# Token sums in twelve steps between evictions, decay earlier, gates spread over the attention

## The chip, the cores and the metric

The kernel runs on one core of a Trainium2 chip. TensorE (PE) multiplies matrices, VectorE (DVE), ScalarE (ACT) and GpSimd (POOL) work on tiles, SyncE (SP) issues most DMAs. Each engine takes its instructions in one fixed order and waits at an instruction until what it reads is written and what it overwrites has been read. The metric is the device time of one execution in microseconds (us). A difference is given against the kernel before.

## The reference, cut to what matters

One layer of a decoder over 1024 tokens of width 1024. A combined projection feeds three mixers: FoX (4 heads, full causal attention with a learned decay), dilated windows (6 heads in 3 groups), and NSA (6 heads in 2 groups; compressed blocks, 8 selected blocks, a window of 512). Each mixer's output is projected, multiplied by a sigmoid gate and summed.

```python
h = rms_norm(x, norm1_g[l])
proj = h @ w_in[l] + b_in[l]          # q, k, v, decay, NSA gates, 3 x 1024 merge gates
y_a = fox_attention(...); y_b = dilated_attention(...); y_c = nsa_attention(...)
g = jax.nn.sigmoid(gates).reshape(B_, S, 3, D)
merged = (g[:, :, 0] * (y_a @ w_pa[l]) + g[:, :, 1] * (y_b @ w_pb[l])
          + g[:, :, 2] * (y_c @ w_pc[l]))
x = x + merged @ w_o[l]
x = x + conv_ffn(rms_norm(x, norm2_g[l]), ...)
# inside FoX: c = cumsum(log_sigmoid(f_logit)); s = q.k * scale + c[t] - c[s]
# inside NSA: kc, vc = gelu(blocks @ w1) @ w2; imp = p_c summed over blocks; top 8 blocks are kept
```

## The kernel before

All products are made in float32 accuracy from two parts, a rounded high part and the low remainder: `mm3` issues three matmuls (L283 to L285) for one product. A weight is loaded by SP (`wr`), its high part (`wh`, `bh`) cast by ScalarE, its low part (`wl`, `bl`) subtracted by GpSimd or VectorE. Two buffers each of `wr`, `wh`, `wl` go round.

The order of the stages is that of `run`. `phase0` norms and transposes the input into `hT` (high and low, two halves of 512 tokens). `proj_va` makes FoX's values and decay logits, `proj_vn` NSA's values and its gate logits, both with tokens as rows: eight token tiles each of 24 matmuls into one of two `dn` banks, evicted by VectorE to `tm` (L668), then cast by ScalarE (L675), its low part made by GpSimd (L676), and stored by SP (L678). `tok_weights` (L635) fills one pair of buffers `bh`, `bl`, so `proj_vn`'s weights follow `proj_va`'s last matmul. Between the two stands `token_sums` (L472 to L495): for the four pairs of row blocks it forms the sums T1 to T4 of a block scheme with fewer products, on 128x512 tiles, seven instructions on VectorE (L483 to L489) and two on GpSimd (L490, L491), and then splits each T into a cast by ScalarE (L493) and a remainder by VectorE or GpSimd (L494). `proj_pairs` uses them for the query, key and value projections; its weights are combined by GpSimd (`su`, L578 to L581) and split (L587, L588).

Fourteen DMAs that GpSimd issues (`dax`, `day`, `dac`, L1772 to L1774) put constant rows of the attention into DRAM buffers; they are released by `last_split`, the low part of the last token weights made so far.

After the pairs, `fox_decay` (L704) turns the decay logits `fa` into the cumulative log decay `fcc` (two activations, some ten VectorE instructions, two small matmuls), and twice `compress_in` and `compress` follow: a projection (KC, then VC), then 48 matmuls of 256 columns over the compression weights `cmp_k_w1` or `cmp_v_w1`.

Then the attention runs. A strip is 128 queries of one head against its keys: score matmuls into `S` (L785, L789; mask L787), row maximum by VectorE (L792), exponent by ScalarE (L800), scaling (L808 to L816), transposes (L857), splits (L863, L864), and products with the values (L886, L887). Ten FoX and dilated heads come first, then for each NSA group a selection (`nsa_select`, L1226: scores of compressed blocks L1242 to L1245, small VectorE instructions L1251 to L1286, transposes L1293, a store into `dax`, which the next loads read back into `q2`, the second operand of L789) and three heads. TensorE's order is written out by a planner, `Flow`: it follows strips and their later steps by a model of the engines, and where none is ready it takes a step of the filler. The filler, `dense_work` (L1317), makes the 24 merge gates (`gate`, L1306): each has 48 matmuls of 512 columns in two `dn` banks, a ScalarE eviction and a DMA. Gates 0 to 20 are taken as soon as there is room, 21 to 23 only behind the attention. Gates' weights come in the order of `weight_list` (L1325): KC, VC, gate 0, 1, and so on. `branch` (L1332) then reads the mixers' outputs (`yh` is cast at L1340), and the merge begins.

## Time and profile before

| what | value |
|---|---|
| median of three runs | 1807.32 us (1804.41 to 1808.73) |
| the profiled execution: time, span | 1807.93 us, 1806.2 us |
| TensorE busy, mean granted clock | 94% of the span, 0.98 |
| first matmul of the pairs, of the compression, of the strips | 104.20, 280.45, 339.50 us |
| last gate matmul, last attention matmul, first of the merge | 810.96, 940.14, 947.29 us |

A view by windows gives the busy time of every engine in a stretch; a view in order of time gives single instructions, and in brackets how long the engine had been idle before one and what released it. An order gives what stands behind what on an engine, and no times.

### The profile page before, as it was taken

The page shows a single profiled execution, that of the slowest core. Times are in us where ns is not written, and L with a number is a line of the kernel's source. Part 1 is how long each engine was busy: PE and PEld are TensorE (multiplying, and loading weights), DVE is VectorE, ACT ScalarE, POOL GpSimd, SP SyncE. Part 2 cuts the span into 40 slices and gives each one's busy share as a digit, 9 for nine tenths or more (in the row PEclk, how much of TensorE's full clock was granted, in tenths as well). Part 3 has the DMA queues.
Part 4 walks back from the last instruction along what each step waited for, and adds up shares of the span by engine and source line. Part 5 has one row for each costly group of instructions (what it writes and reads, how often), then busy time and mean ns, then how long its engine had stood idle before and what let it go on. Part 6 is the DMA issues. An engine that isn't in the chain of part 4 may idle for free.

```text
span 1806.2 us, 24845 instructions
## 1 busy us (share of the span) xinstructions
PE 1691.9 (94%) x8504; PEld 1395.2 (77%) x8504; DVE 1354.0 (75%) x2657; ACT 803.7 (44%) x1638; POOL 468.9 (26%) x334
## 2 busy tenths in 40 slices
...
GB/s 240 71 131 156 130 176 171 184 178 177 192 189 181 69 120 136 68 153 36 8 42 227 208 221 6 18 111 175 186 141 175 179 175 148 135 263 236 204 227 61
DMA packets 224325, 266.52 MB, mean 148 GB/s; under 512 B 20712, under 2 KB 160078, under 8 KB 223990
## 3 DMA queue, kind: packets, MB, share of 16 engines
...
q14 instruction: 60, 0.49, 0.1%
...
## 4 chain that ended last, share of the span: by engine, by line
PE 30%; DVE 15%; issue 5%; DMA 5%; ACT 3%; POOL 2%; SPq 0%; POOLq 0%; DVEq 0%; ACTq 0%
PE dn L284 4%; PE dn L283 4%; PE dn L285 4%; PE S L285 2%; PE S L284 2%; PE S L283 2%; DVE t L1556 2%; DVE u L1614 2%; PE T L284 2%; PE T L283 2%; PE T L285 2%; PE T L857 1%; DVE wl L1493 1%; DVE wh L1493 1%; DVE tl L864 1%
## 5 line engine op out<-in xcount | busy, mean ns | idle before, releaser
L271 POOL TENSOR_TENSOR wl<-wr,wh 128x1024 fp32r<-128x1024 f32 (+2 forms) x50 | 87.9, 1757 | 557.1 <-ACT wh L269 470.8
L283 PE MATMUL dn<-hTh,wh 128*128 128x512 f32 x444 | 179.7, 405 | 0.0
L284 PE MATMUL dn<-hTl,wh 128*128 128x512 f32 x444 | 174.4, 393 | 0.0
L285 PE MATMUL dn<-hTh,wl 128*128 128x512 f32 x416 | 164.0, 394 | 0.0
L800 ACT ACTIVATE p<-S,sm 128x384 f32<-128x384 f32 (+2 forms) x192 | 106.6, 560 | 88.9 <-DVE sm L796 66.6
L864 DVE TENSOR_TENSOR tl<-T,th 128x512 fp32r<-128x512 f32 (+2 forms) x202 | 115.7, 585 | 25.8 <-ACT th L863 24.8
L863 ACT CAST th<-T 128x512 fp32r<-128x512 f32 (+2 forms) x202 | 99.2, 508 | 75.4 <-PE T L857 72.6
L792 DVE TENSOR_REDUCE sm<-S 128x1 f32<-128x384 f32 (+2 forms) x192 | 98.0, 526 | 44.1 <-PE S L789 42.0
L857 PE MATMUL T<-ident,p 128*128 128x128 f32 x610 | 94.8, 279 | 12.1 <-DVE tl L864 5.6
L1556 DVE SCALAR_TENSOR_TENSOR t<-u,ccols,t 128x511 f32<-128x511 f32 (+1 forms) x88 | 96.9, 1101 | 7.5 <-ACT t L1551 6.4
L789 PE MATMUL S<-k,q 114*128 114x384 f32 (+6 forms) x240 | 96.5, 402 | 2.4 <-DMA k<-fcc 1.3
L886 PE MATMUL PV<-th,v 128*128 128x256 f32 (+1 forms) x362 | 95.1, 287 | 1.8 <-DVE yt L903 1.8
L785 PE MATMUL S<-k,q 128*128 128x384 f32 (+2 forms) x240 | 86.1, 359 | 8.4 <-ACT p L800 7.7
L284 PEld LDWEIGHTS dn<-hTl,wh 128*128 128x128 f32 x444 | 84.4, 190 | 12.3
L283 PEld LDWEIGHTS dn<-hTh,wh 128*128 128x128 f32 x444 | 84.3, 190 | 12.1 <-issue 0.6
L887 PE MATMUL PV<-tl,v 128*128 128x256 f32 (+1 forms) x362 | 90.2, 286 | 2.4 <-DVE tl L864 2.4
L285 PEld LDWEIGHTS dn<-hTh,wl 128*128 128x128 f32 x416 | 78.5, 189 | 16.9
L857 PEld LDWEIGHTS T<-ident,p 128*128 128x128 f32 x610 | 70.7, 142 | 21.9 <-DVE p L816 5.0
L887 PEld LDWEIGHTS PV<-tl,v 128*128 128x128 f32 x362 | 70.4, 195 | 6.3 <-DVE tl L864 3.9
L886 PEld LDWEIGHTS PV<-th,v 128*128 128x128 f32 x362 | 70.2, 194 | 5.9 <-DVE yt L903 3.5
L1481 POOL TENSOR_TENSOR su<-wr 128x512 f32<-128x512 f32 x20 | 31.2, 1560 | 142.1 <-DMA wr<-w_up 91.9
L816 DVE TENSOR_SCALAR p<-p,sm,gsig 128x256 f32<-128x256 f32 (+3 forms) x144 | 65.6, 486 | 1.2
...
## 6 DMA issues: line engine op xcount, KB each, us to landing
...
```

The lines of the kernel that those rows point to most:

```text
L283: nc.tensor.matmul(out, st[0], mv[0], start=first, stop=False)
L284: nc.tensor.matmul(out, st[0], mv[1], start=False, stop=False)
L285: nc.tensor.matmul(out, st[1], mv[0], start=False, stop=last)
L789: nc.tensor.matmul(ps[:, 0:wn * P], q[1][0:R, qs], k[1][0:R, cs], start=False, stop=True)
L792: nc.vector.tensor_reduce(mx if ci == 0 else sm[:, 1:2], v, AX.X, ALU.max, negate=True)
L800: nc.scalar.activation(pt[:, 0:m, :].rearrange("p a b -> p (a b)"), v, AF.Exp, bias=mx, accum_out=sm[:, 2 + ci:3 + ci])
L857: nc.tensor.transpose(ps[:, n * P:(n + 1) * P], b, self.ident)
L863: nc.scalar.copy(th[:, cs], ps[:, cs])
L864: nc.vector.tensor_tensor(tl[:, cs], ps[:, cs], th[:, cs].bitcast(F32), ALU.subtract)
L886: nc.tensor.matmul(unit.pv[:, oc], w, th[:, cs], start=first and i == 0, stop=False)
L887: nc.tensor.matmul(unit.pv[:, oc], w, tl[:, cs], start=False, stop=e)
L1556: nc.vector.scalar_tensor_tensor(o, i, cw[2 - sh], o, ALU.mult, ALU.add)
```

## The change

The sums become a generator that yields after T1, after T2, and after T3 with T4, four times: twelve steps. `proj_tok` calls one behind each token tile, released by the tile's eviction and its low part; what is left after both projections is drained then. `constants2` moves ahead of the first projection and `fox_decay` between the two; the fourteen GpSimd issues follow the second projection's last split. Gate 0 and gate 1 are run between `compress_in` and `compress`, and the weight list follows. Gates 2 to 20 are let into the attention only as its strips progress: each strip adds its key blocks and 3 to `prog`, and gate f waits until `prog * 21` has reached `total * (f - 3)`. Gates 21 to 23 stay closed while strips remain.

```diff
@@ -161,6 +161,7 @@
         self.S, self.T, self.PV, self.dn = Ring(3), Ring(2), Ring(1), Ring(2)
         self.p, self.th = Ring(8), Ring(3)
         self.marks = set()
+        self.prog, self.total = 0, 1
         self.vq, self.tq, self.later, self.stores = [], [], [], []
         self.running = False
         self.loads, self.strips, self.filler, self.fn = [], None, None, None
@@ -468,9 +469,9 @@
             self.done = evac(hh, ps)
             F.dn.give(self.done)
 
-    def token_sums(self, pool):
-
-        nc, B = self.nc, {}
+    def token_sums(self, pool, B):
+
+        nc = self.nc
         v, g = nc.vector.tensor_tensor, nc.gpsimd.tensor_tensor
         for n, i, k in (("B11", 0, 0), ("B21", 0, 4), ("B12", 1, 0), ("B22", 1, 4)):
             B[n] = tuple(x[:, k:k + 4] for x in self.hT[i])
@@ -480,19 +481,27 @@
             f = {n: tuple(x[:, i].bitcast(F32) for x in B[n]) for n in B}
             tt = [self.st.tile([P, 2, 512], F32, t) for t in (("sh", "sl"), ("f4", "f4"))[i % 2]]
             r = {n: tt[x // 2][:, x % 2] for x, n in enumerate(("T1", "T2", "T3", "T4"))}
+
+            def split(n, e):
+                nc.scalar.copy(B[n][0][:, i], r[n])
+                e(B[n][1][:, i], r[n], f[n][0], ALU.subtract)
+
             v(r["T1"], f["B12"][0], f["B11"][0], ALU.subtract)
             v(r["T1"], r["T1"], f["B12"][1], ALU.add)
             v(r["T1"], r["T1"], f["B11"][1], ALU.subtract)
+            split("T1", v)
+            yield
             v(r["T2"], f["B22"][0], r["T1"], ALU.subtract)
             v(r["T2"], r["T2"], f["B22"][1], ALU.add)
+            split("T2", g)
+            yield
             v(r["T3"], r["T2"], f["B11"][0], ALU.subtract)
             v(r["T3"], r["T3"], f["B11"][1], ALU.subtract)
             g(r["T4"], f["B21"][0], r["T2"], ALU.subtract)
+            split("T3", v)
             g(r["T4"], r["T4"], f["B21"][1], ALU.add)
-            for n, e in (("T1", v), ("T2", g), ("T3", v), ("T4", g)):
-                nc.scalar.copy(B[n][0][:, i], r[n])
-                e(B[n][1][:, i], r[n], f[n][0], ALU.subtract)
-        return B
+            split("T4", g)
+            yield
 
     def out_qk(self, side, dst, r=1, scale=1.0):
 
@@ -665,25 +674,30 @@
                 self.mm3(ps[:, 0:n], self.toks(self.hT, k, t),
                          (hi[:, k, 0:n], lo[:, k, 0:n]), k == 0, k == 7)
             tm = rawp.tile([P, 274], F32, "tm")
-            nc.vector.tensor_tensor(tm[:, 0:n], ps[:, 0:n], bc[:, 0:n], ALU.add)
-            evac(t, tm)
+            out = nc.vector.tensor_tensor(tm[:, 0:n], ps[:, 0:n], bc[:, 0:n], ALU.add)
+            low = evac(t, tm)
+
+            if self.steps:
+                with self.tc.issue_after(out.ins), self.tc.issue_after(low.ins):
+                    next(self.steps, None)
 
     def v_store(self, t, tm, c0, nh, dsts):
         nc = self.nc
         vs = self.st.tile([P, 4, P], F32R, "v4")
         tv = tm[:, c0:c0 + nh * 64].rearrange("p (h d) -> p h d", h=nh)
         nc.scalar.copy(vs[:, 0:nh, 0:64], tv)
-        nc.gpsimd.tensor_tensor(vs[:, 0:nh, 64:128], tv, vs[:, 0:nh, 0:64].bitcast(F32), ALU.subtract)
+        low = nc.gpsimd.tensor_tensor(vs[:, 0:nh, 64:128], tv, vs[:, 0:nh, 0:64].bitcast(F32), ALU.subtract)
         for (dst, h0, hn) in dsts:
             nc.sync.dma_start(dst[:, t * P:(t + 1) * P, :].rearrange("h p d -> p h d"),
                               vs[:, h0:h0 + hn, :].bitcast(F32))
+        return low
 
     def proj_va(self):
         nc = self.nc
 
         def evac(t, tm):
-            self.v_store(t, tm, 0, 4, [(self.dv["a"], 0, 4)])
             nc.vector.tensor_copy(self.fa[:, :, t], tm[:, 256:260])
+            return self.v_store(t, tm, 0, 4, [(self.dv["a"], 0, 4)])
 
         self.proj_tok(self.va, 260, evac)
 
@@ -692,8 +706,8 @@
         gl = self.early.tile([P, NT, 18], F32, "gl")
 
         def evac(t, tm):
-            self.v_store(t, tm, 0, 4, [(self.dv["s"], 0, 2), (self.dv["w"], 2, 2)])
             nc.vector.tensor_copy(gl[:, t, :], tm[:, 256:274])
+            return self.v_store(t, tm, 0, 4, [(self.dv["s"], 0, 2), (self.dv["w"], 2, 2)])
 
         self.proj_tok(self.tok_weights([(C_VSL, 128), (C_VWN, 146)], 274), 274, evac)
         e = self.early.tile([P, NT, 18], F32, "ge")
@@ -703,7 +717,7 @@
 
     def fox_decay(self):
 
-        nc, ap = self.nc, self.ap
+        nc, ap = self.nc, self.early
         t = lambda n: ap.tile([P, 4, NT], F32, n)
         cm = ap.tile([P, 256], F32, "cm")
         nc.sync.dma_start(cm, self.a["c_main"][:, K_TRI:K_TRI + 256])
@@ -721,7 +735,7 @@
         ps = self.psA.tile([P, 512], F32, "T")
         nc.tensor.matmul(ps[0:32, 0:P], lf.rearrange("p h i -> p (h i)"), tri, start=True, stop=False)
         nc.tensor.matmul(ps[0:32, 0:P], lp.rearrange("p h i -> p (h i)"), ones, start=False, stop=True)
-        cc = ap.tile([32, 4, P], F32R, "fcc")
+        cc = self.nsac.tile([32, 4, P], F32R, "fcc")
         nc.scalar.copy(cc[:, 0], ps[0:32, 0:P])
         nc.vector.tensor_tensor(cc[:, 1], ps[0:32, 0:P], cc[:, 0].bitcast(F32), ALU.subtract)
         nc.vector.tensor_scalar(cc[:, 2], cc[:, 0].bitcast(F32), -1.0, None, ALU.mult)
@@ -762,6 +776,7 @@
 
         nc, ap, F = self.nc, self.ap, self.F
         n = kb1 - kb0 + 1
+        F.prog += n + 3
         sm = ap.tile([P, 8], F32, "sm")
         qs = slice(qi * P, (qi + 1) * P)
         mx, ls = keep or (sm[:, 0:1], sm[:, 4:5])
@@ -1314,19 +1329,22 @@
 
         yield from self.dense_steps(evac)
 
-    def dense_work(self):
-
-        for f in range(24):
+    def dense_work(self, done):
+
+        F = self.F
+        for f in range(done, 24):
             if f == 21:
 
                 yield lambda: INF if self.F.attending else 0.0
+            else:
+
+                yield lambda f=f: INF if F.prog * 21 < F.total * (f - done - 1) else 0.0
             yield from self.gate(f)
 
     def weight_list(self):
         win = self.a["w_in"][0]
         w = lambda c, sc=None: ([win[:, c:c + P]], 8, P, sc)
-        out = [w(C_KC), w(C_VC)]
-        out += [w(C_G + f * P) for f in range(24)]
+        out = [w(C_KC), w(C_G), w(C_VC)] + [w(C_G + f * P) for f in range(1, 24)]
         return out
 
     def branch(self, pool, ys, br):
@@ -1765,16 +1783,20 @@
         self.psA = Pool(self, "psA", {"dn": 2, "S": 3, "T": 2, "PV": 1}, space=PSUM)
         self.start()
         self.phase0()
+        self.constants2()
+        tp = Pool(self, "sums", {})
+        B = {}
+        self.steps = self.token_sums(tp, B)
         self.proj_va()
-        self.constants2()
+        self.fox_decay()
+        self.proj_vn()
         with self.tc.issue_after(self.last_split.ins):
             for i in range(12):
                 nc.gpsimd.dma_start(self.dax[i], a["c_ax"][i])
             nc.gpsimd.dma_start(self.day, a["c_ay"])
             nc.gpsimd.dma_start(self.dac, a["c_ac"])
-        tp = Pool(self, "sums", {})
-        B = self.token_sums(tp)
-        self.proj_vn()
+        for _ in self.steps:
+            pass
         self.early.close()
         pp = Pool(self, "pairs", {})
         self.proj_pairs(B, pp)
@@ -1784,11 +1806,13 @@
                                      "yt": 4, "ce": 2, "csm": 4, "pb": 2})
         self.F = F = Flow()
         self.wspec, self.wloaded, self.wready = self.weight_list(), [], []
-        F.strips, F.filler = self.attention(), self.dense_work()
-        self.fox_decay()
+        F.total = 1138
+        F.strips, F.filler = self.attention(), self.dense_work(2)
         self.ap2 = Pool(self, "att2", {"p": 8})
         for i in range(2):
             fq = self.compress_in(i)
+            for _ in self.gate(i):
+                pass
             self.compress(i, fq)
         with self.tc.manual_schedule(engines={mybir.EngineType.PE}):
             F.run(True)
```

Three places of the orders, before and after. The first is GpSimd between the last token sums and the pairs' `su`; `T2l`, `T4l` are remainders of the sums (L494, after L487), `v` the low parts of token tiles (L676, after L689), L490 and L491 (after L500, L502) sums. Before:

```order
L490 TENSOR_TENSOR f_153_742<-hTh_1_78,f_152_741 128x512
L491 TENSOR_TENSOR f_153_742<-f_153_742,hTl_2_79 128x512
L494 TENSOR_TENSOR T2l_679<-f_152_741,T2h_678 128x512
L494 TENSOR_TENSOR T4l_683<-f_153_742,T4h_682 128x512
L676 TENSOR_TENSOR v_164_813<-tm_811,v_164_813 128x4x64
```

After:

```order
L1795 DMA dax_24_129<-c_ax 16x3200
L1795 DMA dax_25_130<-c_ax 16x3200
L689 TENSOR_TENSOR v_169_801<-tm_798,v_169_801 128x4x64
L500 TENSOR_TENSOR sl_677<-hTh_1_78,sh_676 128x512
L689 TENSOR_TENSOR v_172_842<-tm_839,v_172_842 128x4x64
L502 TENSOR_TENSOR sl_677<-sl_677,hTl_2_79 128x512
L1795 DMA dax_26_131<-c_ax 16x3200
L487 TENSOR_TENSOR T4l_445<-sl_677,T4h_444 128x512
L1795 DMA dax_27_132<-c_ax 16x3200
L689 TENSOR_TENSOR v_177_882<-tm_879,v_177_882 128x4x64
L1795 DMA dax_28_133<-c_ax 16x3200
L1795 DMA dax_29_134<-c_ax 16x3200
```

Sums, splits and the issues, which stood ahead of the sums, now stand between the low parts of the second projection's tiles.

The second is TensorE in the compression of the values; `S` is the product with the compression weights `k`, `dn_3095` gate 2. Before:

```order
L283 MATMUL S_2835<-k_474_2837,p_2817 128x256
L284 MATMUL S_2835<-k_475_2838,p_2817 128x256
L285 MATMUL S_2835<-k_474_2837,p_2818 128x256
L283 MATMUL S_2835<-k_477_2856,p_2821 128x256
L284 MATMUL S_2835<-k_478_2857,p_2821 128x256
L285 MATMUL S_2835<-k_477_2856,p_2822 128x256
```

After:

```order
L286 MATMUL S_2957<-k_489_2978,p_2883 128x256
L284 MATMUL dn_3095<-hTh_1_78,wh_2895 128x512
L285 MATMUL dn_3095<-hTl_2_79,wh_2895 128x512
L286 MATMUL dn_3095<-hTh_1_78,wl_2896 128x512
L284 MATMUL S_2957<-k_492_2997,p_2886 128x256
L284 MATMUL dn_3095<-hTh_1_78,wh_2895 128x512
L285 MATMUL dn_3095<-hTl_2_79,wh_2895 128x512
L286 MATMUL dn_3095<-hTh_1_78,wl_2896 128x512
L284 MATMUL dn_3095<-hTh_1_78,wh_2895 128x512
L285 MATMUL dn_3095<-hTl_2_79,wh_2895 128x512
```

Before, the 48 matmuls of that product stood in a row; now gate 2 stands between them, and gates 0 and 1 ahead of the two products.

The third is TensorE in the second selection; `dn` are gate matmuls, `T` transposes of the selection (L1293, after L1308), L785 to L789 (after L800 to L804) the first strips behind it, L1257 to L1260 scores of compressed blocks. Before:

```order
L283 MATMUL dn_10395<-hTh_3_80,wh_10305 128x512
L1293 MATMUL T_8622<-ident_82,s_1755_8607 16x128 x4
L785 MATMUL S_8643<-k_1714_8393,q_1758_8632 128x256
L787 LDWEIGHTS identb_648
L787 MATMUL S_8643<-mk_645,identb_648 128x128
L284 MATMUL dn_10395<-hTl_4_81,wh_10305 128x512
L285 MATMUL dn_10395<-hTh_3_80,wl_10306 128x512
L283 MATMUL dn_10395<-hTh_3_80,wh_10305 128x512
```

After:

```order
L1260 MATMUL S_8404<-k2c_398,q_1695_8206 128x256
L1257 MATMUL S_8404<-k1c_397,q_1694_8205 128x256
L1258 LDWEIGHTS identb_392
L1258 MATMUL S_8404<-mk_389,identb_392 128x64
L1260 MATMUL S_8404<-k2c_398,q_1695_8206 128x256
L1308 MATMUL T_8439<-ident_82,s_1737_8424 16x128 x4
L800 MATMUL S_8460<-k_1696_8210,q_1740_8449 128x256
L802 LDWEIGHTS identb_392
L802 MATMUL S_8460<-mk_389,identb_392 128x128
L804 MATMUL S_8460<-k_1697_8211,q_1741_8450 128x256
L800 MATMUL S_8471<-k_1696_8210,q_1740_8449 128x256
L802 LDWEIGHTS identb_392
```

The gate matmuls around the transposes are gone: scores, transposes and the first strips follow one another, and the first gate matmul comes four strips later.

## Rows read from the trace of the kernel before

**Rows 1.** The page, part 1: span, then busy us, share and instructions of each engine.

```profile
span 1806.2 us, 24845 instructions
...
PE 1691.9 (94%) x8504; PEld 1395.2 (77%) x8504; DVE 1354.0 (75%) x2657; ACT 803.7 (44%) x1638; POOL 468.9 (26%) x334
```

**Rows 2.** By stage: stretch, us, busy PE PEld DVE ACT POOL (instructions), PEclk, DMA, GB/s.

```profile
45.00:104.20 59.20, 36.07 (x225) 33.12 (x223) 47.77 (x55) 16.32 (x31) 39.98 (x29) 0.77 0.29 78
...
280.45:339.50 59.05, 51.28 (x255) 41.34 (x253) 36.86 (x74) 22.24 (x32) 9.59 (x9) 0.94 0.70 170
339.50:811.00 471.50, 463.05 (x2744) 387.71 (x2744) 329.63 (x1090) 244.62 (x641) 63.54 (x37) 0.99 0.55 150
811.00:940.30 129.30, 99.44 (x650) 81.70 (x648) 107.68 (x318) 73.76 (x210) 1.00 (x1) 0.95 0.06 17
```

**Rows 3.** TensorE in order of time, second token projection and pairs: start, us, line, operation.

```profile
89.69 0.29 PE L283 MATMUL dn<-bh,hTh 128*128 128x274 f32 x1
...
92.87 0.29 PE L284 MATMUL dn<-bl,hTh 128*128 128x274 f32 x1
...
107.17 0.39 PE L283 MATMUL S<-hTh,wl 128*128 128x512 f32 x1
...
108.98 0.39 PE L285 MATMUL S<-hTh,wl 128*128 128x512 f32 x1
```

**Rows 4.** Front in order of time, [idle before <-releaser]; last GpSimd's issues by tile, ns least/median/most.

```profile
39.95 0.68 DVE L483 TENSOR_TENSOR sh<-hTh,hTh 128x512 f32<-128x512 f32 x1
...
58.18 1.76 DVE L489 TENSOR_TENSOR f<-f,hTl 128x512 f32<-128x512 f32 x1
...
84.31 0.59 PE L283 MATMUL dn<-bh,hTh 128*128 128x274 f32 x1 [5.89 <-DVE tm L668]
...
99.32 0.73 POOL L676 TENSOR_TENSOR v<-tm,v 128x256 fp32r<-128x256 f32 x1 [2.32 <-ACT v L675]
...
106.13 1.29 POOL L578 TENSOR_TENSOR su<-wr 128x512 f32<-128x512 f32 x1
...
110.88 0.51 PE L285 MATMUL S<-T3h,wl 128*128 128x512 f32 x1 [0.66 <-DVE wl L588]
...
L1772 POOL DMA_DIRECT2D dax<-c_ax x12: 486/493/671, 21.5 to 38.5; - x12
```

**Rows 5.** Compression: TensorE's waits (us, times, longest), ScalarE in time, a stretch.

```profile
PE S L283 <- ACT k L1188: 2.1, 1, 2.1
...
329.43 1.04 ACT L1188 CAST k<-q 128x1024 fp32r<-128x1024 f32 x1 [3.92 <-DMA q<-cmp_v_w]
...
330.00:340.00 10.00, 7.33 (x32) 6.27 (x32) 3.23 (x5) 2.31 (x5) 0.94 (x1) 0.66 0.62 155
```

**Rows 6.** Attention by stretch, columns as in rows 2, cut where heads begin.

```profile
339.50:544.83 205.33, 202.19 (x1202) 170.20 (x1202) 142.33 (x463) 120.09 (x322) 29.57 (x16) 0.98 0.69 184
544.83:590.60 45.77, 45.77 (x262) 38.44 (x260) 29.72 (x128) 15.41 (x33) 9.16 (x7) 1.00 0.69 190
...
717.65:763.93 46.28, 45.82 (x292) 38.42 (x291) 35.13 (x103) 27.18 (x74) 4.35 (x2) 1.00 0.23 66
763.93:803.47 39.54, 35.94 (x215) 29.57 (x214) 26.76 (x132) 12.19 (x31) 5.13 (x6) 1.00 0.73 188
...
847.50:890.20 42.70, 32.54 (x228) 26.51 (x227) 37.49 (x116) 26.00 (x76) 0.00 (x0) 1.00 0.07 21
890.20:940.30 50.10, 39.07 (x258) 32.35 (x256) 41.69 (x124) 28.71 (x83) 0.00 (x0) 0.94 0.03 7
```

**Rows 7.** Second selection's way through memory: the stretch, and VectorE's next instruction.

```profile
793.00:803.47 10.47, 9.06 (x42) 6.98 (x42) 0.00 (x0) 2.26 (x4) 0.74 (x1) 1.00 0.67 192
...
803.89 0.79 DVE L792 TENSOR_REDUCE sm<-S 128x1 f32<-128x128 f32 x2 [10.92 <-PE S L789]
```

**Rows 8.** End of the attention: TensorE's first merge matmul, and the stretch before it.

```profile
947.29 0.80 PE L283 MATMUL S<-yh,wh 128*128 128x512 f32 x1 [6.74 <-ACT yh L1340]
...
940.30:950.00 9.70, 2.92 (x8) 1.72 (x8) 3.07 (x4) 3.50 (x4) 0.00 (x0) 0.68 0.55 181
```

## The prediction

> **What bounds the kernel now.** The page's first part comes first: TensorE is busy 94% of the span of 1806.2 us [rows 1]. The profiled execution took 1807.93 us in all, 0.6 above the median of 1807.32 (1804.41 to 1808.73), so the sum is made against 1807.9 and the difference is left out. A share of 94% is a mean, so I cut the span at the first matmul of each stage [rows 2]. Four stages then look different. From 45 to 104.2 us (end of the first token projection, the token sums, the second token projection) VectorE works 47.8 of 59.2 us, TensorE 36.1, and at a mean granted clock of 0.77. In the compression stage TensorE is busy 51.3 of 59.05. In the attention up to 811 it is full. From 811 to 940.3, where no gate work is left, it is busy 99.4 of 129.3, and VectorE 107.7.
>
> Busy times of matmuls hold modelled ends, so I also price the order. Eight steps of 512 columns took 1.81 us, 25 of 274 columns 3.18 [rows 3]: 0.226 and 0.127 us each, or 0.416 ns a column and 13 ns a matmul. Transposes are counted twice, as a choice. One gate (48 matmuls of 512 columns) is then 10.9 us. Priced like that, the attention before is 514.5 us of work in 600.8: 442.8 in 471.5 up to 811 (6% over), 71.6 in 129.3 behind it (80% over). What the gates are worth as filler is the difference between these two rates.
>
> **Front: the sums.** Before, VectorE makes the sums in one block that starts at 39.95; the second projection's first evictions are queued behind it, and TensorE stands 5.89 us until the first of them has freed a bank, at 84.31 [rows 4]. A sum of 128x512 takes VectorE 0.68 us alone and 1.76 beside a GpSimd sum or split. The work stays: 28 sums and 8 splits on VectorE, 8 and 8 on GpSimd, 16 casts. By the order 12 of VectorE's stand behind the second projection's first eviction, where 2 stood: 10 at 0.7 to 1.8 us, 7 to 18 us, have left its way. Against that come the decay instructions, now ahead of the first such eviction: 7 adds and some eight small VectorE instructions, two activations and two matmuls, some 4 us by chained waits; and the second weights' low parts share one buffer with the first's, so they wait for a last first-projection tile that now comes later. I take the first eviction 6 to 9 us earlier, at 75 to 78. On SP the constants' and the decay's loads go ahead of the second weights, which wait for their buffers anyway: nothing.
>
> That does not move the pairs as far, because GpSimd becomes late. The 14 `dax`, `day`, `dac` issues, 0.493 us median [rows 4], ran in idle GpSimd time before the block; now they stand between the sums and the preparation of the pair weights `su`, which starts at 106.13 before, and the third product's low weight is waited for at 110.88 [rows 4], so nothing is slack there. Queue after: 8 low parts of 0.73, 7 sums and splits of about 1.7 (1.76 is the nearest row), 14 issues of 0.49 = 5.8 + 11.9 + 6.9 = 24.6 us from some 77 to 79, so `su` starts at 102 to 104: **3 us earlier**. Bounds: with the issues in gaps 7 us earlier; with each tile waiting for the one before, 3 later.
>
> A rule speaks against the new place of the issues. In the row they take 0.49 median and 0.67 at most, the twelve `dax` between 21.5 and 38.5, where VectorE splits the normed input. The Trainium skill ("DMA: Bandwidth & Descriptors", section SWDGE vs HWDGE vs iDMA) says that GpSimd writes descriptors into SBUF state from which a VectorE instruction in a two-port mode locks it out. The row shows little of it; what it would do is the third rival.
>
> **Compression.** Before, TensorE waits there for the cast of the compression weights, 2.1 us in one piece, ScalarE having waited 3.92 for their DMA, and the stretch 330 to 340 runs at a mean clock of 0.66 [rows 5]. By the order it holds 141 dense matmuls and 96 of 256 columns: 31.9 + 11.5 + about 1 = 44.4 us of work in 59.05, so 14.6 lost. After: gates 0 and 1 whole and 45 matmuls of gate 2, that is 237 dense, 96 more, 21.7 us; two stand in the very places of these waits. Work 66.1. I take 4 us still lost (the first strips' loads, the tail of the second compression, which has little filler): stage 70, 11 longer, for 21.7 us of gates that leave the attention: **net -10.8**. Bounds: nothing lost -14.5; half of the loss left -7.5; none recovered, a rival. The gates' result tiles share two buffers with the compression's inputs; the wait for their stores is hidden by a gate's 10.9 us. The decay's move out is in this too.
>
> **Attention.** Without the 21.7 us the old one would be 579.1. After, by the order: gate work in the ten FoX and dilated heads 91 (107 before), in the two selections 7.4 and 0 (before 30.5 and 12.4, and more behind the second), and two gates, 21.7, in each of the six NSA heads (before 33, 37, 18, 13, 0 and 0).
> - FoX and dilated: 205.3 us for 188.5 of work before [rows 6], 1.09; after 173.2, at the same rate 189.
> - NSA heads: the old head nearest to the new ones (25.3 of strips, 17.7 of gates, 717.65 to 763.93) took 46.28 for 43.0, 1.076 [rows 6]. After: strips of 157.4 in all and 130.2 of gates, 287.6, times 1.076 = 309.5. The last two took 42.7 and 50.1 without gates [rows 6]; they would take 52 and 56 with 21.7 each, so their gates cost 15 of 43.
> - Selections: 45.8 and 39.5 before. In the second VectorE works 26.8 us, all of it ahead of 793 [rows 6, 7], then stands 10.92 while the selection is stored and read back into `q2`; TensorE meanwhile worked on gates, 9.06 of 10.47 us at full clock [rows 7]. After there is no filler in the second, little in the first; the VectorE work and the round trip stay: 39.5 each, 79.
>
> Sum 577.5 against 579.1: **-1.6**. So the gain of the filled tail is nearly paid back by two selections that stand empty. On SP the gates' weight loads, now later, stand among the heads' loads and wait for a buffer: nothing while a gate lies between two of them, up to a gate's 10.9 us at one head if not. Bounds: rates of 1.04 and 1.03 in heads give 555; the other end is the second rival.
>
> **End.** Before, the first merge matmul waits 6.74 us for the casts of the last attention output [rows 8]; ten matmuls of gate 23 now fill a part of that hole. It ends at the same cast: 0 (-2; +3 if the merge weights, whose buffers the gates now hold longer, come late).
>
> **Sum.** -3 - 10.8 - 1.6 + 0 = -15.4: **1792.5**; with what the bounds of the terms add alike, 1778 to 1803.
>
> **Rivals.** *First, the spread works everywhere at the rate of the full body:* only 3% are lost outside the selections: (173.2 + 287.6) x 1.03 + 79 = 553.6, -25.5; total 1807.9 - 3 - 10.8 - 25.5 = 1768.6. For it: TensorE was busy 202.2 of 205.3 us in the first ten heads and throughout the first selection [rows 6]. Against: VectorE needs 37.5 of 42.7 us in a head without gates [rows 6].
>
> *Second, slower: the gate by progress leaves holes.* After, 14 stretches of strips alone exceed 3 us of work, 90.7 us together (before 6, 92.9). If all run like the old tail, 1.8 x 90.7 + (492.8 - 90.7) x 1.065 = 591.5, 12.4 more than 579.1. And TensorE leaves each selection cold: in the hole of 6.7 us before the merge the clock falls, 0.68 over 940.3 to 950, the lower level of 1.2 GHz for two thirds of it [rows 8]. At two thirds of 10 us a stretch, half the rate costs 3.4 us each, 6.8 for both, by the 0.66 of [rows 5] over one such stretch. Together +19.2: 1807.9 - 3 - 10.8 + 19.2 = 1813.3. It decides from some +14 in the attention. Against: most of these stretches are short and have gates on both sides. The Trainium skill ("TensorE: Matmul & The Clock Gate", section HAM oscillation) has the same rule, that repeated holes make each following stretch start cold; the trace agrees at the merge (0.68) and shows full clock where gates fill the round trip.
>
> *Third, the front's issues are stretched* like VectorE's sums beside GpSimd, 1.76 for 0.68, 2.6 times: 14 x 0.8 = 11 more on GpSimd, `su` 8 late instead of 3 early: 1792.5 + 11 = 1803.5.
>
> *Fourth, the change does not do what it says in the compression:* weights bound the stage, the gates only lengthen it by their 21.7: 1792.5 + 10.8 = 1803.3.
>
> **How the numbers follow.** Forecast 0.48, first rival 0.19, second 0.18, third 0.07, fourth 0.08. The likeliest gives 1792. About 0.2% (3.6 us) is what a measurement of this kernel can tell from no change, 1803.7 to 1810.9. Faster: the forecast less 0.02, the first, half of the third and fourth = 0.73. Slower: two thirds of the second, 0.12. Same: the rest, 0.15. The range takes the first rival's middle and the lower half of the second: 1765 to 1809; what is left out is the faster third of the first (0.07) and the slower part of the second (0.12).
>
> **What would show it.** First second-projection eviction at 75 to 78, `su` at 102 to 104, pairs' start some 3 us earlier; first strip 70 us behind the first compression matmul; selections of 38 to 41 us each with VectorE idle about 11; NSA heads of 47 to 56; first merge matmul 6 to 8 us behind the last attention matmul. It is wrong if the selections take their old time or much less, if heads with two gates take over 1.12 of their priced work, or if the compression stage grows by more than 18.

## The result

The changed kernel took 1817.52 us, median of five runs (1814.68 to 1822.67), against 1805.22 (1804.41 to 1808.73) for five runs of the kernel before: a ratio of 1.0067 with a 95% interval of 1.0046 to 1.0088. It is slower by 12 us where 15 us less were forecast.

The profiled execution of after took 1817.52 us, 9.6 more than that of before (1807.93), so the stages are compared in these two. First the page of after, part 1 (columns as in [rows 1]):

```profile
span 1815.7 us, 24851 instructions
...
PE 1693.4 (93%) x8504; PEld 1398.5 (77%) x8504; DVE 1352.2 (74%) x2657; ACT 805.2 (44%) x1639; POOL 470.6 (26%) x334
```

Busy times are those of before to within 2 us: the work is the same, and 8.0 of the 9.5 us that the span grew by are idle time of TensorE. By stage, columns as in [rows 2] (stretch, us, busy PE PEld DVE ACT POOL, PEclk, DMA, GB/s); the stretch 283.05 to 350.95 is the compression:

```profile
45.00:104.20 59.20, 44.67 (x258) 40.83 (x259) 49.45 (x70) 20.43 (x38) 45.21 (x42) 0.80 0.41 114
...
283.05:350.95 67.90, 67.69 (x346) 56.71 (x345) 33.47 (x62) 26.60 (x38) 13.44 (x10) 1.00 0.84 213
```

| stage (from first matmul to first matmul) | before | after | difference | forecast |
|---|---|---|---|---|
| start to compression | 280.45 | 283.05 | +2.6 | -3 |
| compression | 59.05 | 67.90 | +8.9 | +11 |
| attention, to its last matmul | 600.64 | 598.10 | -2.5 | -23.3 (-21.7 and -1.6) |
| to the merge's first matmul | 7.15 | 9.65 | +2.5 | 0 |
| rest | | | -1.8 | 0 |

The error of 25 us is 5.6 in the front, 20.8 in the attention, 2.5 at the merge, less 2.1 in the compression and 1.8 in the rest. Two statements of what stands ahead of the prediction were wrong. Gates 21 to 23, which the planner emits behind the attention, stand by the orders of both kernels among the NSA strips. And the last gate matmul of before starts at 818.39, not at 810.96 (12 more matmuls, 2.7 us):

```profile
818.39 0.48 PE L285 MATMUL dn<-hTh,wl 128*128 128x512 f32 x1
```

The prediction's 71.6 us of strips alone stand behind this matmul by the order, so they took 121.4 us and not 129.3: 1.70 times their price, not 1.8.

**Where the attention's time is.** In the two tables of windows below the attention is cut at the first score matmul of a head, a selection taken with the head behind it: ten heads; selection 1 and head 1; head 2; head 3; selection 2 and head 4; head 5; head 6. After:

```profile
350.95:548.45 197.50, 189.52 (x1134) 159.06 (x1132) 145.47 (x459) 114.98 (x314) 27.35 (x15) 0.97 0.64 171
548.45:639.75 91.30, 73.18 (x449) 61.48 (x447) 63.71 (x237) 38.92 (x102) 7.28 (x7) 0.91 0.37 103
639.75:694.75 55.00, 51.92 (x326) 43.96 (x324) 41.94 (x123) 30.37 (x80) 5.60 (x3) 1.00 0.34 86
694.75:752.45 57.70, 51.88 (x309) 43.86 (x307) 41.44 (x110) 29.00 (x79) 5.75 (x3) 0.97 0.39 115
752.45:841.45 89.00, 68.57 (x416) 56.68 (x415) 61.94 (x238) 36.50 (x98) 6.90 (x6) 0.90 0.41 109
841.45:893.45 52.00, 51.50 (x324) 43.23 (x323) 38.71 (x115) 29.38 (x83) 2.40 (x1) 1.00 0.11 32
893.45:949.05 55.60, 53.95 (x344) 44.24 (x342) 44.64 (x123) 31.37 (x87) 3.24 (x2) 1.00 0.10 32
```

The same for the changed kernel without its gate by progress (run e2, below), which holds the same gates 2 to 23 there:

```profile
350.34:550.84 200.50, 198.72 (x1202) 167.94 (x1201) 142.24 (x459) 118.35 (x318) 29.69 (x16) 1.00 0.66 176
550.84:655.04 104.20, 104.20 (x602) 87.27 (x600) 67.02 (x237) 45.98 (x112) 16.37 (x10) 1.00 0.46 126
655.04:719.34 64.30, 60.74 (x366) 50.49 (x363) 50.74 (x128) 32.63 (x85) 7.66 (x3) 1.00 0.47 127
719.34:758.84 39.50, 39.10 (x260) 32.17 (x259) 34.03 (x106) 25.20 (x73) 2.50 (x1) 1.00 0.20 55
758.84:839.54 80.70, 67.25 (x395) 54.74 (x394) 59.60 (x238) 35.21 (x99) 3.69 (x6) 0.92 0.38 102
839.54:883.14 43.60, 35.49 (x229) 29.13 (x228) 37.59 (x116) 26.34 (x77) 0.00 (x0) 0.92 0.08 21
883.14:932.84 49.70, 37.70 (x257) 31.30 (x255) 41.67 (x124) 28.46 (x83) 0.00 (x0) 0.97 0.03 6
```

Take a stretch less its PE busy time: that is TensorE's idle time in it, its holes. After, in order: 8.0, 18.1, 3.1, 5.8, 20.4, 0.5, 1.7, together 57.6. In e2: 1.8, 0, 3.6, 0.4, 13.4, 8.1, 12.0, together 39.3. The gate by progress did fill the tail, as meant: the last two heads lost 17.9 us of idle time. It opened 25.1 in the two selections with their heads, and 11.6 in the ten heads and head 3. In all TensorE is idle 18.3 us more and busy 2.6 less, and the attention is 15.7 longer than in e2. The new holes are mostly long waits: after has nine over 1.5 us in the attention, 39.3 us together, e2 five with 10.3. Four of the nine are the selections' own chains (TensorE in order of time; in brackets the idle time before, and its releaser):

```profile
579.89 1.02 PE L1308 MATMUL T<-ident,s 128*16 128x128 f32 x4 [8.40 <-DVE s L1301]
...
586.53 0.55 PE L804 MATMUL S<-k,q 114*128 114x256 f32 x1 [5.27 <-DMA q<-dax]
...
779.68 1.02 PE L1308 MATMUL T<-ident,s 128*16 128x128 f32 x4 [7.68 <-DVE s L1301]
...
786.28 0.58 PE L804 MATMUL S<-k,q 114*128 114x256 f32 x1 [5.23 <-DMA q<-dax]
```

26.6 us in two places. In each, TensorE first waits for VectorE's selection chain, then for its result's way through memory. Before, gate matmuls lay beside these chains; a selection adds nothing to `prog`, so no threshold is reached while one runs: by the order the first holds 33 matmuls of a gate let in earlier, and the second none.

**Where the front's time is.** After, ScalarE, GpSimd and TensorE at the end of the second token projection:

```profile
101.22 0.41 ACT L688 CAST v<-tm 128x256 fp32r<-128x256 f32 x1 [2.84 <-DMA dv_w<-v]
105.25 0.41 ACT L688 CAST v<-tm 128x256 fp32r<-128x256 f32 x1 [3.63 <-DMA dv_w<-v]
```

```profile
105.75 0.72 POOL L689 TENSOR_TENSOR v<-tm,v 128x256 fp32r<-128x256 f32 x1 [2.83 <-ACT v L688]
106.43 0.52 POOL L1795 DMA_DIRECT2D dax<-c_ax  x1
...
107.43 0.49 POOL L1797 DMA_DIRECT2D dac<-c_ac  x1
107.93 1.27 POOL L587 TENSOR_TENSOR su<-wr 128x512 f32<-128x512 f32 x1
```

```profile
111.24 0.79 PE L284 MATMUL S<-T3h,wl 128*128 128x512 f32 x1 [4.51 <-ACT wl L596]
```

The last two value casts wait 2.84 and 3.63 us until a store has left one of the two `v4` buffers. The last low part waits for the cast; three issues of half a microsecond and then `su`, at 107.93 where [rows 4] has 106.13, stand behind it on GpSimd; and the third product (T3h) waits 4.51 us for its low weight. From 78.71, where the first of these low parts starts, to 107.93 GpSimd works 22.8 us and waits 6.4, of which 3.6 are for the last two casts.

### The profile page after: what moved, and what is told of

The parts are those of the page before. It is cut to its first block, busy times and chain, and to the rows that moved or that the text cites. A ratio compares the mean times of both kernels' runs of the same rounds, so it can differ in the third digit from the quotient of the medians.

```text
span 1815.7 us, 24851 instructions
## 1 busy us (share of the span) xinstructions
PE 1693.4 (93%) x8504; PEld 1398.5 (77%) x8504; DVE 1352.2 (74%) x2657; ACT 805.2 (44%) x1639; POOL 470.6 (26%) x334
## 5 line engine op out<-in xcount | busy, mean ns | idle before, releaser
L804 PE MATMUL S<-k,q 114*128 114x384 f32 (+6 forms) x240 | 97.5, 406 | 10.5 <-DMA q<-dax 10.5
L800 PE MATMUL S<-k,q 128*128 128x384 f32 (+2 forms) x240 | 86.9, 362 | 9.0 <-ACT p L815 9.0
L286 PEld LDWEIGHTS dn<-hTh,wl 128*128 128x128 f32 x416 | 78.8, 189 | 16.6
L872 PEld LDWEIGHTS T<-ident,p 128*128 128x128 f32 x610 | 71.3, 143 | 20.4 <-DVE tl L879 7.1
L286 PE MATMUL S<-blk,wh 128*128 128x512 f32 x156 | 61.8, 396 | 3.6 <-POOL wh L1511 2.6
```

The source lines that it names most:

```text
L286: nc.tensor.matmul(out, st[1], mv[0], start=False, stop=last)
L804: nc.tensor.matmul(ps[:, 0:wn * P], q[1][0:R, qs], k[1][0:R, cs], start=False, stop=True)
L872: nc.tensor.transpose(ps[:, n * P:(n + 1) * P], b, self.ident)
```

## Experiments

Each run's ratio is against the kernel before on the same chip (medians 1803.7 to 1806.0). A profiled run can lie off its kernel's median, mostly by under 6 us, in e14 by 9.0 (1802.21 against 1793.18). So stages carry such differences too: the ten heads, in one and the same order, took 197.5 us in after and 194.2 in e5. The verdicts go by the medians.

**The three parts alone.** e1: before, with gates 0 and 1 in the compression.

```diff
-        F.strips, F.filler = self.attention(), self.dense_work()
+        F.strips, F.filler = self.attention(), self.dense_work(2)
@@
             fq = self.compress_in(i)
+            for _ in self.gate(i):
+                pass
             self.compress(i, fq)
```

> The kernel before with one part of the change alone: gates 0 and 1 between the compression's input and its product, the weight list in that order, gates 2 to 20 let in at once as before. Theory A (gates that leave the attention save less than their price, because the attention then runs out of filler earlier): by the order the strips behind the last gate grow from 71.7 to 81.0 us of priced work; 81.0 x 1.8 + 411.8 x 1.065 = 584.3 us for the attention against 600.8, the compression stage 59 to 68: net -7.6, some 1797.6 us. Theory B (they save their full 21.7 us, and the whole loss of the change sits in the gate by progress): attention 579, stage 68, net -12.9, some 1792.3 us.

Measured 1799.26 us, 0.9976 [0.9965, 0.9988]. The stage is 70.31 us, the attention 583.87: 21.7 us of gates left it, and it became 16.8 shorter, not 21.7 (18.3 by the 582.38 of e2, which has the same order there).

e2: the changed kernel without the gate by progress.

```diff
-            else:
-
-                yield lambda f=f: INF if F.prog * 21 < F.total * (f - done - 1) else 0.0
             yield from self.gate(f)
```

> The changed kernel without the gate by progress: gates 2 to 20 are let in at once. Theory A: the attention takes 584 us as with the compression part alone, the front costs 2.6 us up to the compression: 1800. Theory B: attention 579, 1795. Both: faster than the change by 17 to 22 us; if the gate by progress were harmless and the loss came from the front or the compression, it would stay at 1815 to 1818.

Measured 1799.60 us, 0.9971 [0.9959, 0.9982]. So the gate by progress costs 17.9 us between the medians of e2 and after, 15.7 in the attention (598.10 against 582.38) and 3.1 at the merge (9.65 against 6.56).

e3: the front alone, which is e2 without the gates in the compression.

```diff
-        out = [w(C_KC), w(C_G), w(C_VC)] + [w(C_G + f * P) for f in range(1, 24)]
+        out = [w(C_KC), w(C_VC)]
+        out += [w(C_G + f * P) for f in range(24)]
@@
-        F.strips, F.filler = self.attention(), self.dense_work(2)
+        F.strips, F.filler = self.attention(), self.dense_work(0)
@@
-            for _ in self.gate(i):
-                pass
```

> The kernel before with the front part alone: sums in twelve steps, constants and decay moved up, the fourteen GpSimd issues behind the second projection's split; compression and attention as before. Theory A and B: the second projection ends 3 us earlier, the pairs' third product starts 1.7 us later, the compression 2.6 us later; the decay no longer stands in the compression stage, which gives 1 to 2 back: 1806 to 1808. A rival, that the front is worth its 3 us: 1802.

Measured 1803.52 us, 0.9988 [0.9972, 1.0003], which can't be told from no change. The compression starts at 281.76, 1.3 later than before, and takes 54.14 instead of 59.05, since the decay no longer stands in it.

e4: before with the gate by progress alone, for all the gates up to 20 (the diff leaves out the counter's start and the function's header).

```diff
+        F.prog += n + 3
@@
+            else:
+
+                yield lambda f=f: INF if F.prog * 21 < F.total * (f - 3) else 0.0
             yield from self.gate(f)
@@
+        F.total = 1138
```

> The kernel before with the gate by progress alone (thresholds as in the change; gates 0 to 3 open from the start). Theory A: the attention of the change, 598, with 21.7 us more of gates in its first heads: about 617 to 621 and 2.5 more at its end, some 1821 to 1827 us. Theory B: 1827. A rival, that the gate by progress does harm only where two gates have already left: 1805 to 1810.

Measured 1835.92 us, 1.0179 [1.0161, 1.0198], more than expected. By the orders the ten heads hold as much gate work as before (107.3 and 106.6 us, priced as in the prediction), and took 218.8 us where [rows 6] has 205.3.

**Cold clock or idle time.** The granted clock of after in the selections with their heads is 0.91 and 0.90 in the windows above. e5: after, with matmuls of no use around each selection's transposes, which keep TensorE busy there (`idle(n)` makes n matmuls of 512 columns into a `dn` bank that nobody reads).

```diff
             F.T.take()
+            idle(34)
             pst = self.psA.tile([P, 512], F32, "T")
@@
                 F.pe(256)
+            idle(26)
```

> The changed kernel with matmuls whose result nobody reads in the two holes of each selection: 34 of 512 columns (7.7 us) ahead of the transposes of the selection, 26 (5.9 us) behind them. They add no useful work. In the changed kernel the stretches of the selections and of the head behind each run at a mean clock of 0.90 to 0.91, 34 us at the lower level in all. Theory C (the cold clock behind the empty selections is a main part of what the gate by progress costs): the clock goes to 1.0 there and 5 to 12 us come back: 1805 to 1812. Theory D (the strips there are bound by VectorE and the round trip, the clock costs little): clock 1.0, and 1815 to 1819, as the change.

Measured 1818.63 us, 1.0078 [1.0064, 1.0092], the time of after. The two selections with their heads in e5:

```profile
545.57:636.97 91.40, 86.08 (x508) 71.82 (x507) 63.54 (x237) 38.76 (x102) 7.25 (x7) 0.98 0.37 102
749.91:838.81 88.90, 81.66 (x475) 67.87 (x474) 61.36 (x238) 36.55 (x98) 6.90 (x6) 0.96 0.41 110
```

The clock rises from 0.91 and 0.90 to 0.98 and 0.96, TensorE's busy time by 26 us, and the lengths stay (91.3 and 89.0 in after). The unused matmuls hardly held the selections up: the transposes start 31.4 and 28.2 us into the two stretches, 31.4 and 27.2 in after. The holes are latencies of other work; the colder clock in them is a sign, and no cost of it shows (the two intervals leave room for some 4 us).

**Gates for the selections.** e6: after, with progress counted in the selections.

```diff
                 yield lambda: max(sel[r].ready, F.S.avail())
+                F.prog += 10
                 q = sel[r].t
@@
-        F.total = 1138
+        F.total = 1138 + 240
```

> The changed kernel with progress counted in the selections too (10 for each of their 24 steps, the total raised by 240): by the order each selection gets two gates, 21.7 us, the FoX and dilated heads 76.7 instead of 91.0, later heads a little less. Theory E (empty selections are what the gate by progress costs): their holes of 13 us each are filled for nothing, -15 to -20 against the change: 1798 to 1803. Theory A (a gate is worth what the stretch that it leaves loses; the FoX and dilated heads give back little, 3 us for 15.6 of gates): -3 to -8: 1810 to 1815.

Measured 1832.99 us, 1.0153 [1.0138, 1.0167]: a miss, on the wrong side. Each selection got its two gates (43.4 us with its head), and still waits of 9.57 and 8.61 us for `q` stand behind them; the ten heads, with 14 us less of gates than in after, took 206.6 us instead of 197.5.

**The front's ring.** e7 is e2 with three `v4` buffers; e8 is e7 with the `dax`, `day` and `dac` issues ahead of `fox_decay`.

```diff
@@ e7
-        self.st = Pool(self, "stage", {"f4": 2, "b8": 2, "v4": 2}, side="right")
+        self.st = Pool(self, "stage", {"f4": 2, "b8": 2, "v4": 3}, side="right")
@@ e8
         self.proj_va()
-        self.fox_decay()
-        self.proj_vn()
         with self.tc.issue_after(self.last_split.ins):
...
+        self.fox_decay()
+        self.proj_vn()
```

> The changed kernel without the gate by progress (1799.6 in its own runs) and with three buffers instead of two for the token tiles' value stores. Theory F (the last value casts wait for a store's landing, 2.8 and 3.6 us, and hold up the low parts and the preparation of the pair weights behind them on GpSimd): the preparation starts 2 us earlier than 107.9, the wait of 4.5 us for the third product shrinks as much: some 1797.5. Theory G (the fourteen issues of GpSimd hold it up): no change, 1799 to 1800.

> As the one with three buffers, and the fourteen GpSimd issues go back ahead of the sums, behind the first projection's last split. Theory F: another 1 to 2 us at the pairs, since three of the issues stand right ahead of the preparation: 1796. Theory G: here first the wait of 4.5 us goes, 3 to 4 us less than without: 1796. They differ in the run with three buffers alone; a rival to both, that the second projection itself ends too late for it: 1799 in both.

e7: 1798.76 us, 0.9954 [0.9936, 0.9971]; e8: 1799.80, 0.9967 [0.9953, 0.998]. With a third buffer the third product of the pairs comes at 108.02, in e2 at 111.10:

```profile
108.02 0.50 PE L284 MATMUL S<-T3h,wl 128*128 128x512 f32 x1 [1.17 <-ACT wl L596]
```

The compression starts at 279.58, against 282.47 in e2. `su` starts at 104.66, where after has 107.93, with the issues in the same place: the stores' buffers held the front. In the time it is too little for the intervals of e2 and e7 to separate, and against before the compression starts 0.9 us earlier, not 3. e8's move, from which a gain was expected too, added nothing: there the last value cast waits 3.35 us for a store again, in spite of three buffers, and `su` starts at 106.70.

**The planner's costs.** e9: after, with the planner's costs of VectorE, ScalarE and small instructions raised towards the trace's.

```diff
-        return (self.D.op(ready + self.LAT, 0.07 + n * 1.04e-3) if eng == "D"
-                else self.A.op(ready + self.LAT, 0.12 + n * 0.85e-3))
+        return (self.D.op(ready + self.LAT, 0.15 + n * 1.04e-3) if eng == "D"
+                else self.A.op(ready + self.LAT, 0.17 + n * 0.85e-3))
@@
-        return self.D.op(ready + self.LAT, 0.07 + n * 0.6e-3)
+        return self.D.op(ready + self.LAT, 0.2 + n * 0.7e-3)
@@
-            ready = self.D.op(ready + 0.1, 0.07)
+            ready = self.D.op(ready + 0.1, 0.16)
@@
-            e = F.psum(m * P + 100, r, "A")
+            e = F.psum(m * P + 330, r, "A")
```

> The changed kernel, whose planner counts VectorE's and ScalarE's instructions as the trace has them: row operations 0.15 + 1.04 ns a column instead of 0.07, scaling 0.2 + 0.7 ns a column instead of 0.07 + 0.6, small ones 0.16 instead of 0.07, the exponent with its accumulator read 0.2 more. Gates and thresholds stay. Theory M (with the gates shut the planner sends strips ahead of VectorE, and TensorE then waits in its order, as at the value products for `yt`): those waits shrink, the attention gets 8 us shorter, some 1809. Theory N (stretches of strips alone take 1.8 times their price whatever the order among the strips): by the order stretches of strips alone over 3 us grow from 91 to 144 us of work: 1818 to 1830.

Measured 1874.74 us, 1.0379 [1.0361, 1.0397], worse than anything expected. By the order the stretches of strips alone did grow, as expected, but why that costs so much was not followed further.

**Amount and grain of the filler.** e11: e7 with gates 19 and 20 held back whole, to `prog` 796 and 910, so that the two last heads get some.

```diff
+            elif f in (19, 20):
+
+                yield lambda f=f: INF if F.prog < (796, 910)[f - 19] else 0.0
             yield from self.gate(f)
```

> The changed kernel without the gate by progress and with three value buffers (1798.8 in its own runs), but gate 19 waits for the end of the strips of the third NSA head and gate 20 for the start of the fifth: by the order the second and third NSA head lose 26.5 and 10.6 us of gates, the last two get 20.1 and 18.1. Theory A (gates cost what exceeds the room that a stretch has anyway): second head 64 to 45, third 39.5 to 39, the last two 43 and 50 to 52 and 55, the merge 2 later: 0 to -4, 1795 to 1799. The rule of the prediction (filler costs its price times 1.07 wherever it stands, and a stretch without filler 1.8): 64 to 49, 39.5 to 45, 43 and 50 to 51 and 52: +5, 1804.

Measured 1807.39 us, 1.0012 [1.0001, 1.0023]: 8.6 more than e7, above both expectations. The last two heads took 50.9 and 53.7 with 20.1 and 18.1 us of gates, 43.6 and 49.7 in e2 with none.

e13: e7 with a threshold for each of a gate's 16 steps. e14: e13, with progress counted in the selections (`F.total` 1270).

```diff
@@ e13
-            yield from self.gate(f)
+            for need in self.gate(f):
+                n += 1
+                yield lambda need=need, n=n, f=f: INF if f < 21 and (F.prog + 80) * 304 < F.total * n else need()
@@ e14
                 yield lambda: max(sel[r].ready, F.S.avail())
+                F.prog += 10
@@
             F.marks.add(f"sel{g}")
+            F.prog += 40
```

> On the same base the gates 2 to 20 are let in by progress again, but step by step: each of their 304 steps (three matmuls) has its own threshold, instead of one for a whole gate. Selections have no filler (2.0 us each). By the order the strips-only stretches over 3 us come to 69.9 us, of which 24 in the selections. Theory P (the harm of the gate by progress is its grain: a gate is taken in one piece, then strips run bare): ten heads 184, selections 78, six heads 300: 562 us for the attention against 577, some 1784. Theory Q (bare strips are not it; shut gates let the strips run into each other): as the change, 1808 to 1818.

> As the one in fine grain, with progress counted in the selections too: 10 for each of their steps, 40 at the transposes that begin the way through memory, and the last threshold at 87% of the whole. By the order the two selections hold 27.8 and 27.2 us of gates, the ten heads 74.7, the six NSA heads 18, 18, 18, 21, 13, 11. Theory P: (74.7 + 81.9) x 1.1 = 172 for the ten heads, 42 for each selection, 256.6 x 1.07 = 275 for the six heads: 531 us against 577, some 1753. Theory Q: 1805 to 1818. Theory E (empty selections alone are the harm): 20 to 25 less than in fine grain without them.

e13: 1801.53 us, 0.9976 [0.9964, 0.9987]; e14: 1793.18, 0.9934 [0.9913, 0.9955], so e13 lies between its two theories, and e14 is 8.4 us under it where its third had 20 to 25. (In e13 77 gate matmuls, 17.4 us, fall behind the attention, into the 17.6 us before the merge, and from there to the end it takes 853.3 us where after has 857.0.)

e15: as e14, but gates are taken as soon as there is room in the ten heads, and spread by steps from the first selection on; e16: e7 with every gate ahead of the strips, for the strips' own time.

```diff
@@ e15
-                yield lambda need=need, n=n, f=f: INF if f < 21 and (F.prog + 80) * 304 < F.total * n else need()
+                yield lambda need=need, n=n, f=f: INF if f < 21 and F.prog - 454 < (n - 172) * 5.45 else need()
@@ e16
+        for f in range(2, 24):
+            for _ in self.gate(f):
+                pass
+        F.filler = iter(())
```

> On the base with three value buffers: gates are let in at once in the ten FoX and dilated heads (104.6 us of them by the order, as without thresholds), and from the first selection on step by step by progress, the selections counted: 21.7 and 21.1 us in the selections, 14, 14, 13, 19, 13, 8 in the six NSA heads. Theory R (each stretch of strips has a time of its own that gates do not lengthen until they exceed its room; the ten heads took 192 to 200 us with 75 to 107 us of gates): ten heads 200, first selection and head 89, then 52, 45, 84, 45, 50: 565 us against 577, some 1787. Theory Q (where the gates stand matters little): 577 to 583, 1797 to 1803.

> On the same base all gates are made ahead of the strips, some 229 us more there; the attention runs without a single gate. It gives each stretch's own time. Theory R: ten heads 180 to 195, first selection and head 80 to 87, the other heads 52, 40, 75 (with its selection), 43, 49: some 520 us for 264 of priced work, and 1970 in all. The prediction's rate of 1.8 for bare strips: ten heads 147, all of it 475, 1925.

e15: **1780.88 us**, 0.9872 [0.985, 0.9893], the fastest kernel here, 22.8 us under the kernel before on the same chip (1803.68), and faster than either theory said. e16: 1955.05 us (one execution), between its two theories; its attention, with no gate in it, took 509.9 us:

```profile
576.52:1086.42 509.90, 377.81 (x2285) 311.64 (x2284) 405.97 (x1403) 266.19 (x778) 10.88 (x15) 0.85 0.35 91
```

The strips alone thus leave TensorE idle for 132 us, and 228.9 us of gates lengthen them by 72.5 us in e2, by 55.9 in e15; in after 226.5 us do so by 88.2. The attention of e15, columns and cuts as above:

```profile
346.79:549.29 202.50, 199.37 (x1201) 168.40 (x1199) 143.53 (x462) 118.57 (x319) 29.67 (x16) 0.99 0.65 174
549.29:633.49 84.20, 79.05 (x473) 64.97 (x471) 64.84 (x234) 38.60 (x103) 9.20 (x7) 0.98 0.42 116
633.49:689.99 56.50, 47.16 (x292) 38.62 (x291) 47.28 (x131) 30.20 (x82) 6.21 (x2) 0.97 0.48 131
689.99:736.49 46.50, 43.08 (x271) 35.84 (x269) 37.34 (x106) 26.28 (x73) 2.38 (x1) 0.96 0.21 58
736.49:819.69 83.20, 81.76 (x494) 67.17 (x494) 62.92 (x236) 39.14 (x103) 10.21 (x8) 1.00 0.44 124
819.69:863.79 44.10, 43.87 (x286) 35.66 (x286) 38.81 (x116) 28.24 (x80) 2.66 (x2) 1.00 0.12 37
863.79:912.49 48.70, 43.74 (x293) 35.67 (x291) 41.22 (x123) 29.56 (x84) 1.01 (x1) 1.00 0.07 20
```

Idle: 3.1, 5.2, 9.3, 3.4, 1.4, 0.2, 5.0, together 27.7. Selections and tail are both covered. Head 5 took 44.1 with 13.1 us of gates in it, 43.6 with none in e2: so much of them is free there. Against e2 the attention is 16.6 us shorter: 11.6 of idle time, 5.0 of busy time.

The amounts by stretch had been chosen by a theory that each stretch has room for so much gate work, and that more is paid in full. Two runs kept the amounts, to within some 4 us a stretch, and changed the grain. e17: after, let in by steps; e18: e15, let in by whole gates.

```diff
@@ e17
-                yield lambda f=f: INF if F.prog * 21 < F.total * (f - done - 1) else 0.0
-            yield from self.gate(f)
+            for n, need in enumerate(self.gate(f)):
+                yield lambda need=need, n=n, f=f: INF if f < 21 and F.prog * 336 < F.total * ((f - done - 1) * 16 + n - 8) else need()
@@ e18
+                yield lambda f=f: INF if F.prog - 454 < ((f - done) * 16 + 8 - 172) * 5.45 else 0.0
+            yield from self.gate(f)
```

> The changed kernel with its gates let in step by step (16 steps a gate) instead of gate by gate, each step's threshold centred on the old one of its gate. Amounts of gate work by stretch stay nearly those of the changed kernel (95 in the ten heads, 25 in the first selection with its head, 23, 21, 24, 18, 15 in the following stretches, against 91, 29, 22, 22, 22, 22, 20); strips alone for over 3 us come to 60 us instead of 91. Theory of the distribution (it matters only how much gate work each stretch gets): the attention stays within 3 us of 598, the time at 1813 to 1819. Theory of the lump (a whole gate let in at once fills the next gaps and leaves those after them empty): most of the 15 us goes, attention 583 to 588, time 1800 to 1806.

> The kernel of the run eager then fine (1780.9, attention 565.8) with the same progress line but whole gates let in, each at the threshold of its middle step. Amounts by stretch stay: 105 in the ten heads (105 there), 37 in the first selection and head (36), 11 and 11 (14, 13), 43 in the second selection and head (40), 14 and 9 (13, 8); strips alone for over 3 us come to 92 us instead of 45. Theory of the distribution: 1779 to 1784, attention 564 to 569. Theory of the lump: 1790 to 1797, attention 575 to 582.

e17: 1815.35 us, 1.0053 [1.0035, 1.0071]; e18: 1818.26, 1.0077 [1.0058, 1.0096]. Neither theory holds for both: finer steps gave after 2 us, inside the intervals, and whole gates cost e15 37. Amounts do not explain that: by the orders each of e18's ten heads holds the gate work of e15's to within 1.4 us, and together they took 215.9 us, 12.9 of them idle, where e15 took 202.5. The attention of e17 in one window, then that of e18, and the ten heads of e18:

```profile
351.27:945.98 594.71, 535.79 (x3265) 447.21 (x3264) 438.33 (x1403) 308.56 (x837) 58.38 (x35) 0.95 0.43 113
```

```profile
347.61:951.94 604.33, 548.54 (x3297) 456.33 (x3295) 436.76 (x1403) 309.16 (x840) 59.40 (x36) 0.96 0.41 113
...
347.61:563.51 215.90, 202.98 (x1197) 170.80 (x1195) 145.99 (x459) 117.17 (x318) 29.68 (x16) 0.97 0.61 163
```

Length less busy time, for the kernels that differ in grain and in whether a selection counts as progress:

| TensorE idle in the attention, us | whole gates | steps |
|---|---|---|
| selections don't count | after 57.6 | e17 58.9, e13 60.7 |
| selections count | e6 65.1, e18 55.8 | e14 39.7, e15 27.7 |

Of these kernels only those with both have clearly fewer holes. (e13 holds 67 gate matmuls less in its attention than after, e17 21 less; the profile of e14 is of its slowest run.) But e2, which lets gates in at once, has 39.3, and e14, whose steps are metered from the first head on, is no better; nor do the intervals separate its time from that of e7, which has its front and no meter. Only e15 goes below, which in effect leaves the ten heads unmetered. If a selection doesn't count, almost nothing is let in while it runs, however small the portions (2.7 and 2.0 us in e17, which has the waits of after again: 8.25 and 5.81, 7.44 and 6.98 us). If it counts but gates come whole, a gate can be used up in the first gaps, and a later wait then finds none: so I read the waits of e18, 8.65 us for `q`, 5.57 and 3.55 in the ten heads for `yt`. Of the 38.6 us between the attentions of e18 and e15, 28 are idle time; the other 10.4 are longer busy time at a mean clock of 0.96 instead of 0.99, and whether the clock makes them was not tried.

## Why the prediction was wrong

Most of the 25 us is one term, the price of gate work in the attention. The gates that left for the compression gave back 18.3 us there instead of 21.7 (before to e2), and spreading the others by progress cost 15.7 instead of gaining 1.6 (e2 to after).

**Front, -3, measured +2.6.** The sums did leave the evictions' way: the first eviction starts at 77.74 (forecast 75 to 78, before 83.8), the second projection's last matmul at 100.98 (before 104.07). The step that failed is GpSimd's queue, which was summed as if its work were always ready: `su` came at 107.93, not at 102 to 104. The work was about as summed (22.8 us for 24.6, two of the issues having gone before); 6.4 us of waits stood in it. It had left out the ring of the two `v4` buffers, which paces the tiles by their stores once evictions follow one another faster; e7 confirms it by undoing it. The slow bound (each tile waiting for the one before, 3 later) has the right size. The issues, the third rival, took 0.49 to 0.52 us each in the rows shown, and none over 0.67: not stretched. The Trainium skill ("DMA: Bandwidth & Descriptors", SWDGE vs HWDGE vs iDMA) names the lock by which they could be; nothing of it shows here, with VectorE's sums beside them.

**Compression, net -10.8, measured -7.9 to -12.9 by how the attention's part is counted.** The stage was right: 67.90 for 70, with PE busy 67.69 of it at full clock, so the old waits are gone. The other half, 21.7 us in the attention, was 16.8 (e1) to 18.3 (e2): -21.7 + 8.9 = -12.9 by the prediction's way of counting, -7.9 by e1's, -9.4 by e2's. The gates taken out had stood partly in holes. The fourth rival (weights bound the stage) is refuted by that busy share, and by a growth of 8.9 where it had 21.7; part of the gain is the decay's, 4.9 us in e3, 2.4 with the gates (70.31 in e1, 67.87 in e2).

**Attention, -1.6, measured +15.7.** The step that failed is the price of a gate: the strips' work plus the gates' work, times one rate per kind of stretch. It gave the ten heads 189 (measured 197.5), head 3, by its rate, 50.6 (57.7, or 1.23 of its priced work, past the 1.12 that was to show the prediction wrong), and the selections with their heads 177 (180.3). By the orders, priced as in the prediction, the ten heads from e2 to after gave up 15.6 us of gate work and became 3.0 shorter, which is no more than such a stretch varies by; the first selection with its head gave up 34.7 and became 12.9 shorter. The same gates cost 8.4 and 5.9 us for 21.7 and 19.5 in the last two heads, which had been forecast well (52 and 56; measured 52.0 and 55.6). So the tail's gain was sized rightly, and the give-back was missed: gates that leave a covered stretch bring little, because the strips still take their own time there (the attention without a gate, e16, took 509.9 us). The forecast of single selections of 38 to 41 us failed in itself (32.1 and 27.9 to the next head's first matmul): the wait for `q` falls behind the next head's first matmul, so part of a selection lies in that head.

**The second rival** had the mechanism, holes that a gate by progress leaves, and at 1813.3 came nearest. Its sum is not confirmed, though: it charged 6.8 us to the cold clock, which e5 removed without any gain, and it priced stretches of strips alone (at 1.8, where 1.70 was measured), by which e4 (72 us in such stretches over 3 us) should have beaten e2 (104). The Trainium skill ("TensorE: Matmul & The Clock Gate", HAM oscillation) says that repeated holes make the following stretches start cold; the clock of 0.90 and 0.91 in after agrees, and by e5 no price of it shows here.

**End, 0, measured +2.5.** Ten matmuls of gate 23 run behind the last attention matmul, as forecast, but in their own time:

```profile
951.28 0.39 PE L286 MATMUL dn<-hTh,wl 128*128 128x512 f32 x1
958.70 0.80 PE L284 MATMUL S<-yh,wh 128*128 128x512 f32 x1 [7.03 <-ACT yh L1358]
```

They run 2.5 us beyond the last attention matmul, but that alone need not delay the cast of `yh`, for which the merge waits: `yt` is evicted 0.7 us behind that matmul (0.8 before). What is late is SP, which reads the outputs back (`gr`). Before, it issues the first read 1.84 us behind the last attention matmul; after, 4.56, because the load of a merge weight stands ahead of it. That load waits for a buffer until the low part of another weight (`wl`) is made, behind its cast (`wh`), and the cast waits for one of the last gate matmuls. SP before; then ScalarE, GpSimd and SP after, and SP's wait (us in total, times, longest):

```profile
941.98 1.03 SPq L1339 DMA_DIRECT2D gr<-dy_a  x2
...
951.53 0.51 ACT L270 CAST wh<-wr 128x384 fp32r<-128x384 f32 x1 [1.81 <-PE dn L285]
...
952.12 0.99 POOL L272 TENSOR_TENSOR wl<-wr,wh 128x384 fp32r<-128x384 f32 x1 [23.22 <-ACT wh L270]
...
953.14 0.37 SPq L255 DMA_DIRECT2D wr<-w_pa  x1
953.61 0.96 SPq L1357 DMA_DIRECT2D gr<-dy_a  x2
...
SPq L255 <- POOL wl L272: 2.4, 1, 2.4
```

So the bound of +3 that the prediction gave (merge weights that come late because the gates hold their buffers longer) came true, and the 0 was wrong. This is read from the trace; no run moved the load.
